# Hybrid Mamba-2 and attention step on one core: skip weights as whole rows, two first products side by side, a stacked step product, squares summed by TensorE

## The chip, the cores and the metric

The kernel runs on one core of a Trainium2 chip. The metric is the device time of one execution in microseconds (us), as the median of several. TensorE multiplies matrices, VectorE (DVE), ScalarE (ACT) and GpSimd (POOL) work on elements, and SyncE (SP) issues the DMAs, all of them on one queue.

## The reference, cut to what matters

One step of a two-layer decoder: layer 0 is a Mamba-2 mixer and an MLP, layer 1 is sliding-window attention over shared keys and values and an MLP. 1104 columns go through it together: 1024 prompt tokens, 64 sample tokens (8 sequences of 8) and 16 meta tokens, each of width 1024. The change lies in the start of the mixer:

```python
def rmsnorm(x, w):
    xf = xf * lax.rsqrt(jnp.mean(xf * xf, axis=-1, keepdims=True) + EPS)
    return (xf * w).astype(x.dtype)

def mamba_mixer(h, ...):
    zxbcdt = rmsnorm(h, norm_w) @ w_in            # 1024 -> 2048 z, 4096 x/B/C, 32 dt
    conv = conv_b
    for k in range(CONV_K):                       # 4 taps, per channel
        conv = conv + xpad[:, k:k + L] * conv_w[k]
    xbc = jax.nn.silu(conv)
    dt = jax.nn.softplus(dt_raw + dt_bias)        # the step, one per head
    y, h_new = ssd_scan(xs, dt, a_neg, bm, cm, h0)
    y = y + d_skip[head] * xs                     # the skip weights, 32 numbers
    out = gated_group_rmsnorm(y, z, gate_w) @ w_out
```

## The kernel before

Everything is held with features on the 128 partitions and tokens along the columns. The 1104 columns are cut into three chunks (`CH`): c0 and c1 of 384 columns, c2 of 336; the work on them goes in the order c2, c0, c1 (`CORD`). A width of 1024 is eight k tiles (`KT`).

Products of fp32 accuracy are made from parts. A weight or an activation is split into a high part (rounded to fp32r, by ScalarE) and a low part (the difference, by VectorE or GpSimd), and `mm3` (L179 to L181) runs three TensorE products for each k tile: high by high, high weight by low input, low weight by high input. `wunit` loads a weight tile of 512 KB (L160), casts it (L164, ScalarE) and subtracts (L165, GpSimd); it has two raw buffers and six buffers for parts.

`mixer` begins layer 0. `load_h` loads the input, four DMAs of 128x2x384 (336 for c2) fp32 numbers for each chunk (L284). `sums_x` squares them on ScalarE (L295), adds the squares of two k tiles on VectorE (L296) and sums over the partitions with a product by a matrix of 1/1024 in plain fp32 (L297); the squares go through five small buffers (`n1`). `rstd_x` makes the norm from the sums, with a logarithm (L303) and an exponential (L305) on ScalarE, each behind a table load. `norm_x` scales the eight k tiles (L316, VectorE), casts them to high parts (L317, ScalarE) and subtracts for the low parts (L319, even tiles on VectorE, odd ones on GpSimd) into the buffer `S`. The norms of c0 and c1 are written together, behind the sums of both.

A conv unit is one weight tile with its 128 output channels. `conv_mm` multiplies one chunk by it (24 products into one PSUM bank, of which a ring of three is used here) and copies the result out on ScalarE (L513, L515, L517). `conv_rest` does the taps (L533, L536), a tanh and the last product of the SiLU. The first two units are B and C of group 0; each takes c2, then c0, then c1. After them come `dt_product` (72 products with 32 output rows, the step before its bias), the units x0 and x1, `dt_path` (softplus and the running sums of the step) and the state-space groups: eight times `ssd`, 9 blocks each, with the weight loads and products of the next group (`group_in`) between its blocks. The skip weights are held as one column for each pair of heads (`dcol`, L378), read by L631 in `ssd`.

The order of the instructions on each engine is not the order of the code. A scheduler with a model of the machine orders them when the program is built; on the chip each engine works through its list in order and waits on semaphores. Eight hardware semaphores are shared in turn by SyncE's DMAs, so an issue can wait for the DMA eight places before it.

## Time and profile before

| | |
|---|---|
| time, median of 3 runs | 2992.69 us (2989.01 to 2993.91) |
| the profiled execution | 2977.05 us, span 2975.3 us |
| TensorE, share of the span | 96% |
| VectorE | 66% |
| ScalarE | 49% |
| GpSimd | 48% |
| mean granted TensorE clock | 0.984 of full speed |
| moved by DMA | 346.37 MB, mean 116 GB/s |

The span runs from the first to the last instruction; the profiled execution's time holds 1.75 us more. The three timed runs lie 12 to 17 us above the profiled execution. A busy TensorE is not TensorE at its peak, since its records overlap.

### The profile page before, as it was taken

The page shows a single profiled execution, that of the slowest core. Times are in us where ns is not written, and L with a number is a line of the kernel's source. Part 1 is how long each engine was busy: PE and PEld are TensorE (multiplying, and loading weights), DVE is VectorE, ACT ScalarE, POOL GpSimd, SP SyncE. Part 2 cuts the span into 40 slices and gives each one's busy share as a digit, 9 for nine tenths or more (in the row PEclk, how much of TensorE's full clock was granted, in tenths as well). Part 3 has the DMA queues.
Part 4 walks back from the last instruction along what each step waited for, and adds up shares of the span by engine and source line. Part 5 has one row for each costly group of instructions (what it writes and reads, how often), then busy time and mean ns, then how long its engine had stood idle before and what let it go on. Part 6 is the DMA issues. An engine that isn't in the chain of part 4 may idle for free.

```text
span 2975.3 us, 50874 instructions
## 1 busy us (share of the span) xinstructions
PE 2842.1 (96%) x19750; PEld 2728.4 (92%) x19750; DVE 1956.7 (66%) x3157; ACT 1455.1 (49%) x2770; POOL 1424.9 (48%) x1247
## 2 busy tenths in 40 slices
PE   5999999989999989999999999999988999999998
PEld 4998998979999989999999998887878999999998
DVE  5787787775565575454466766776788545366675
ACT  5455555555454465545333336566654444433333
POOL 4476666663323214444255555455543444435562
PEclk8999999999999999999999999999998999999999
DMA  3344444454212224343634312223232444543332
GB/s 126 75 120 121 126 119 120 122 149 139 68 64 71 87 71 152 134 154 124 254 131 134 115 50 65 66 74 105 86 108 97 145 136 149 186 172 128 130 110 75
DMA packets 197545, 346.37 MB, mean 116 GB/s; under 512 B 28648, under 2 KB 130920, under 8 KB 194728
## 3 DMA queue, kind: packets, MB, share of 16 engines
q1 hardware_dynamic: 197304, 343.13, 36.0%
q8 instruction: 155, 2.54, 0.4%
q14 instruction: 86, 0.70, 0.1%
HBM read 252.92 MB, written 91.12 MB: 116 GB/s over the span
## 4 chain that ended last, share of the span: by engine, by line
PE 46%; DVE 9%; ACT 4%; issue 3%; POOL 2%; DMA 1%; DVEq 0%; SPq 0%; POOLq 0%; ACTq 0%
PE g L179 4%; PE g L180 3%; PE g L181 3%; PE mc L179 3%; PE mc L181 3%; PE mc L180 3%; PE ma L179 3%; PE ma L180 3%; PE ma L181 3%; PE md L181 2%; PE md L180 2%; PE mb L179 2%; PE mb L180 2%; PE md L179 2%; PE mb L181 2%
## 5 line engine op out<-in xcount | busy, mean ns | idle before, releaser
L179 PE MATMUL g<-S,w 128*128 128x384 f32 (+3 forms) x1656 | 560.7, 339 | 16.9 <-DVE hh L729 4.8
L165 POOL TENSOR_TENSOR w<-raw,w 128x1024 fp32r<-128x1024 f32 x140 | 344.8, 2465 | 459.8 <-ACT w L164 386.6
L180 PE MATMUL g<-S,w 128*128 128x384 f32 (+3 forms) x1656 | 561.3, 339 | 3.7 <-DVE S L319 3.4
L181 PE MATMUL g<-S,w 128*128 128x384 f32 (+3 forms) x1656 | 556.0, 336 | 0.0
L859 POOL TENSOR_TENSOR w<-s,w 128x384 fp32r<-128x384 f32 (+1 forms) x240 | 324.1, 1354 | 387.1 <-ACT w L858 381.2
L179 PEld LDWEIGHTS g<-S,w 128*128 128x128 f32 (+1 forms) x1656 | 314.8, 190 | 26.3 <-issue 7.0
L859 POOL TENSOR_TENSOR w<-raw,w 128x384 fp32r<-128x384 f32 (+1 forms) x180 | 225.4, 1255 | 227.7 <-ACT w L858 204.4
L180 PEld LDWEIGHTS g<-S,w 128*128 128x128 f32 (+1 forms) x1656 | 314.8, 190 | 8.9 <-DVE S L319 4.4
L181 PEld LDWEIGHTS g<-S,w 128*128 128x128 f32 (+1 forms) x1656 | 314.8, 190 | 4.9 <-issue 2.6
L858 ACT CAST w<-s 128x384 fp32r<-128x384 f32 (+1 forms) x240 | 134.7, 562 | 243.2 <-PE ma L181 67.8
L179 PE MATMUL ma<-S,w 128*128 128x276 f32 (+1 forms) x736 | 213.4, 290 | 4.7 <-DVE us L1059 3.9
L180 PE MATMUL ma<-S,w 128*128 128x276 f32 (+1 forms) x736 | 212.8, 289 | 0.9 <-DVE S L823 0.9
L181 PE MATMUL ma<-S,w 128*128 128x276 f32 (+1 forms) x736 | 212.8, 289 | 0.0
L164 ACT CAST w<-raw 128x1024 fp32r<-128x1024 f32 x140 | 146.4, 1046 | 120.6 <-PE g L180 57.8
L729 DVE TENSOR_TENSOR hh<-hh,g 128x384 f32<-128x384 f32 (+2 forms) x264 | 134.3, 530 | 67.7 <-PE g L181 67.1
L536 DVE SCALAR_TENSOR_TENSOR fm<-xp,cv,fm 128x1024 f32<-128x1024 f32 x96 | 163.2, 1701 | 23.4 <-ACT fm L517 22.8
L858 ACT CAST w<-raw 128x384 fp32r<-128x384 f32 (+1 forms) x180 | 100.5, 561 | 151.7 <-PE mc L181 47.9
L179 PEld LDWEIGHTS ma<-S,w 128*128 128x128 f32 x736 | 139.1, 189 | 5.8 <-ACT w L858 5.7
L180 PEld LDWEIGHTS ma<-S,w 128*128 128x128 f32 x736 | 139.1, 189 | 1.1 <-DVE S L823 1.1
L181 PEld LDWEIGHTS ma<-S,w 128*128 128x128 f32 x736 | 138.9, 189 | 0.0
L179 PE MATMUL mc<-S,w 128*128 128x276 f32 (+1 forms) x464 | 134.4, 290 | 2.7 <-DVE rx L888 1.4
L181 PE MATMUL mc<-S,w 128*128 128x276 f32 (+1 forms) x464 | 134.0, 289 | 0.0
(469 smaller groups left out, 8840.3 us busy)
## 6 DMA issues: line engine op xcount, KB each, us to landing
raw<-in_w_up_dram SPq DMA_DIRECT2D x64, 512.0 KB
raw<-in_w_in_dram SPq DMA_DIRECT2D x48, 512.0 KB
raw<-in_w_downs_dram SPq DMA_DIRECT2D x64, 384.0 KB
ab<-acs_d SPq DMA_DIRECT2D x64, 256.0 KB
S<-t_d SPq DMA_DIRECT2D x18, 828.0 KB
S<-t_e SPq DMA_DIRECT2D x18, 816.0 KB
t_d<-rx SPq DMA_DIRECT2D x12, 1104.0 KB
t_e<-rx SPq DMA_DIRECT2D x12, 1088.0 KB
```

What stands on the lines that cost most here:

```text
L164: nc.scalar.copy(out=wh, in_=raw)
L165: nc.gpsimd.tensor_tensor(out=wl, in0=raw, in1=wh.bitcast(F32), op=ALU.subtract)
L179: mm(out=out, lhsT=wh, rhs=xh, start=(first and k == 0), stop=False)
L180: mm(out=out, lhsT=wh, rhs=xl, start=False, stop=False)
L181: mm(out=out, lhsT=wl, rhs=xh, start=False, stop=(k == n - 1))
L536: nc.vector.scalar_tensor_tensor(out=acc[:, :SEQ], in0=xp[:, k:k + SEQ], scalar=cv[:, j, k:k + 1], in1=acc[:, :SEQ], op0=ALU.mult, op1=ALU ...
L729: nc.vector.tensor_tensor(out=hv, in0=hv, in1=pt[:, :n], op=ALU.add)
L858: nc.scalar.copy(out=t[:, 0], in_=src)
L859: nc.gpsimd.tensor_tensor(out=t[:, 1], in0=src, in1=t[:, 0].bitcast(F32), op=ALU.subtract)
```

## The change

Five things. (1) The 32 skip weights are loaded as one row of 128 bytes to each of 128 partitions (`drow`), and GpSimd picks the 16 columns of each half; before, two DMAs read them with a stride, 64 partitions by 16 single numbers each. The input loads of c1 are written ahead of the mixer's constants. (2) For c0 and c1 the squares are no longer added in pairs on VectorE; each goes to TensorE, 16 products in place of 8. c2 keeps the addition. (3) `conv_mms` runs B and C side by side, k tile by k tile, into two banks. (4) `dt_product` stacks high and low weights in one tile of 64 columns (`wa`) and the raw weights and zeros in another (`wb`): two products for a k tile in place of three, with 64 output rows; `dt_path` adds the two halves while it transposes, by a matrix of two stacked identities (`two`). (5) The copy of 120 rows of the value cache from input to output, which has no inputs from the kernel, is held until the last up-projection weight of layer 0 has been issued.

```diff
--- before.py
+++ after.py
@@ -284,7 +284,7 @@
             self.nc.sync.dma_start(out=hp[kp], in_=self.i["x"][:, 2 * kp:2 * kp + 2, o:o + n])
         return hp
 
-    def sums_x(self, c, hp, tag):
+    def sums_x(self, c, hp, tag, add=False):
 
         nc = self.nc
         n = CH[c][1]
@@ -293,8 +293,11 @@
             sq = [self.n1("xsq")[:, :n] for _ in range(2)]
             for j in range(2):
                 nc.scalar.activation(out=sq[j], in_=h[:, j], func=AF.Square)
-            nc.vector.tensor_tensor(out=sq[0], in0=sq[0], in1=sq[1], op=ALU.add)
-            nc.tensor.matmul(out=ms[:, :n], lhsT=self.ones_d, rhs=sq[0], start=(kp == 0), stop=(kp == 3))
+            if add:
+                nc.vector.tensor_tensor(out=sq[0], in0=sq[0], in1=sq[1], op=ALU.add)
+            for j in range(1 if add else 2):
+                nc.tensor.matmul(out=ms[:, :n], lhsT=self.ones_d, rhs=sq[j], start=(kp + j == 0),
+                                 stop=(kp == 3 and (add or j == 1)))
         return ms[:, :n]
 
     def rstd_x(self, mss):
@@ -374,26 +377,30 @@
         nc.scalar.mul(out=self.cv[:, :, 0:5], in_=self.cv[:, :, 0:5], mul=0.5)
 
         self.dcol = mp.tile([P, 16], F32, name="dcol")
+        drow = mp.tile([P, 32], F32, name="drow")
+        nc.sync.dma_start(out=drow, in_=i["a_d_skip"].broadcast_to([P, 32]))
         for h in range(2):
-            nc.sync.dma_start(
-                out=self.dcol[64 * h:64 * h + 64, :],
-                in_=i["a_d_skip"].rearrange("o (t h) -> o h t", h=2)[:, h].broadcast_to([64, 16]),
-                allow_slow_non_contiguous=True)
+            hs = slice(64 * h, 64 * h + 64)
+            nc.gpsimd.tensor_copy(out=self.dcol[hs], in_=drow[hs].rearrange("p (t h) -> p h t", h=2)[:, h])
 
     def dt_product(self, mp, xs):
+
         nc, i = self.nc, self.i
         raw = self.raw([P, KT, 32])
         nc.sync.dma_start(out=raw, in_=i["w_dt"])
-        wh, wl = (self.wtile([P, KT, 32]) for _ in range(2))
-        nc.scalar.copy(out=wh, in_=raw)
-        nc.vector.tensor_tensor(out=wl, in0=raw, in1=wh.bitcast(F32), op=ALU.subtract)
-        draw = self.fm([32, T], "draw")
+        wa, wb = (self.wtile([P, KT, 64]) for _ in range(2))
+        nc.vector.memset(wb[:, :, 32:64].bitcast(F32), 0.0)
+        nc.scalar.copy(out=wa[:, :, 0:32], in_=raw)
+        nc.vector.tensor_tensor(out=wa[:, :, 32:64], in0=raw, in1=wa[:, :, 0:32].bitcast(F32), op=ALU.subtract)
+        nc.scalar.copy(out=wb[:, :, 0:32], in_=raw)
+        draw = self.fm([64, T], "draw")
         for c in CORD:
             o, n = CH[c]
-            pt = self.gps()
-            self.mm3(pt[:32, :n], [(wh[:, k], wl[:, k]) for k in range(KT)],
-                     [(xs[c][0][:, k, :n], xs[c][1][:, k, :n]) for k in range(KT)])
-            nc.scalar.copy(out=draw[:, o:o + n], in_=pt[:32, :n])
+            pt = self.gps()[:64, :n]
+            for k in range(KT):
+                nc.tensor.matmul(out=pt, lhsT=wa[:, k], rhs=xs[c][0][:, k, :n], start=(k == 0), stop=False)
+                nc.tensor.matmul(out=pt, lhsT=wb[:, k], rhs=xs[c][1][:, k, :n], start=False, stop=(k == KT - 1))
+            nc.scalar.copy(out=draw[:, o:o + n], in_=pt)
         return draw
 
     def dt_path(self, mp, draw):
@@ -413,10 +420,16 @@
         nc.sync.dma_start(out=an, in_=i["a_log"].broadcast_to([P, 32]))
         nc.scalar.activation(out=an, in_=an, func=AF.Exp)
         nc.vector.tensor_scalar(out=an, in0=an, scalar1=-1.0, scalar2=None, op0=ALU.mult)
+
+        two = mp.tile([64, 32], F32, name="two")
+        for h in range(2):
+            hs = slice(32 * h, 32 * h + 32)
+            nc.gpsimd.tensor_copy(out=two[hs], in_=self.ident[hs, hs])
         tps = ps.tile([P, 512], F32, tag="tp", name="tp")
         for t in range(9):
             n = P if t < 8 else 80
-            nc.tensor.transpose(tps[:n, t * 32:(t + 1) * 32], draw[:, t * P:t * P + n], self.ident[:32, :32])
+            nc.tensor.matmul(out=tps[:n, t * 32:(t + 1) * 32], lhsT=draw[:, t * P:t * P + n], rhs=two, start=True,
+                             stop=True)
 
         def full(f):
             f(slice(0, P), slice(0, 8))
@@ -503,12 +516,31 @@
 
     def conv_mm(self, unit, c, xs):
 
-        nc = self.nc
-        j, (wh, wl), xp, acc = unit
-        o, n = CH[c]
+        wh, wl = unit[1]
+        n = CH[c][1]
         pt = self.gps()
         self.mm3(pt[:, :n], [(wh[:, k], wl[:, k]) for k in range(KT)],
                  [(xs[c][0][:, k, :n], xs[c][1][:, k, :n]) for k in range(KT)])
+        self.conv_out(unit, c, pt)
+
+    def conv_mms(self, units, c, xs):
+
+        n = CH[c][1]
+        pts = [self.gps() for _ in units]
+        mm = partial(self.nc.tensor.matmul, skip_group_check=True)
+        for k in range(KT):
+            xh, xl = (x[:, k, :n] for x in xs[c])
+            for (j, (wh, wl), *_), pt in zip(units, pts):
+                mm(out=pt[:, :n], lhsT=wh[:, k], rhs=xh, start=(k == 0), stop=False)
+                mm(out=pt[:, :n], lhsT=wh[:, k], rhs=xl, start=False, stop=False)
+                mm(out=pt[:, :n], lhsT=wl[:, k], rhs=xh, start=False, stop=(k == KT - 1))
+        for unit, pt in zip(units, pts):
+            self.conv_out(unit, c, pt)
+
+    def conv_out(self, unit, c, pt):
+        nc = self.nc
+        j, w, xp, acc = unit
+        o, n = CH[c]
         m = min(n, SEQ - o)
         nc.scalar.copy(out=xp[:, 3 + o:3 + o + m], in_=pt[:, :m])
         if m < n:
@@ -1215,8 +1247,9 @@
         for b in range(NB):
             nc.sync.dma_start(out=o["v_s"][b, 120:128, ds], in_=self.vt[8 * b:8 * b + 8, 8, ds])
         if pr == 0:
-            nc.sync.dma_start(out=o["v_s"][:, 0:120].rearrange("b s d -> b (s d)"),
-                              in_=i["cache_v"][:, 8:128].rearrange("b s d -> b (s d)"))
+            with self.tc.issue_after(self.last_raw):
+                nc.sync.dma_start(out=o["v_s"][:, 0:120].rearrange("b s d -> b (s d)"),
+                                  in_=i["cache_v"][:, 8:128].rearrange("b s d -> b (s d)"))
 
     def keys_values(self, pr, xs, ap, buf, ps):
         yield from self.keys(pr, xs, ap, buf)
@@ -1702,20 +1735,18 @@
         hp = {2: self.load_h(2)}
         us = [self.conv_unit(0, nm) for nm in ("B", "C")]
         hp[0] = self.load_h(0)
+        hp[1] = self.load_h(1)
         self.mixer_consts(mp)
-        hp[1] = self.load_h(1)
-        ms2 = self.sums_x(2, hp[2], "cb")
+        ms2 = self.sums_x(2, hp[2], "cb", True)
         rs2 = self.rstd_x([ms2])[0]
         xs[2] = self.norm_x(2, hp[2], rs2)
         ms0 = self.sums_x(0, hp[0], "st")
         ms1 = self.sums_x(1, hp[1], "y")
-        for u in us:
-            self.conv_mm(u, 2, xs)
+        self.conv_mms(us, 2, xs)
         rs0, rs1 = self.rstd_x([ms0, ms1])
         for c, rs in ((0, rs0), (1, rs1)):
             xs[c] = self.norm_x(c, hp[c], rs)
-            for u in us:
-                self.conv_mm(u, c, xs)
+            self.conv_mms(us, c, xs)
         draw = self.dt_product(mp, xs)
         ux = self.conv_unit(0, "x0")
         fm["B"], fm["C"] = (self.conv_rest(u) for u in us)
```

What the scheduler makes of it, at three places. First SyncE's list at the very start. xt is the input, raw a weight tile, cv the conv weights and states, dtbias and an the step's bias and decay. Before:

```order
L160 DMA raw<-in_w_in_dram 128x1024 x2
L284 DMA xt<-in_x_dram 128x2x384 x4
L373 DMA cv<-in_cv_dram 128x928
L378 DMA dcol<-in_a_d_skip_dram 64x16x1 x2
L284 DMA xt<-in_x_dram 128x2x384 x4
L411 DMA dtbias<-in_a_dt_bias_dram 128x32
L413 DMA an<-in_a_log_dram 128x32
L1218 DMA out_dram<-in_cache_v_dram 8x2x15360
L386 DMA raw<-in_w_dt_dram 128x256
```

Now:

```order
L160 DMA raw<-in_w_in_dram 128x1024 x2
L284 DMA xt<-in_x_dram 128x2x384 x8
L376 DMA cv<-in_cv_dram 128x928
L381 DMA drow<-in_a_d_skip_dram 128x32
L418 DMA dtbias<-in_a_dt_bias_dram 128x32
L420 DMA an<-in_a_log_dram 128x32
L390 DMA raw<-in_w_dt_dram 128x256
```

The four loads of c1 have moved ahead of the conv weights and the skip weights, and the copy of the value cache has left this part of the list.

Second, ScalarE's list from the squares of c1 to the norm of c0 (xsq the squares, S<-xt the casts, xms the sums, n the norm). Before:

```order
L295 ACTIVATE xsq<-xt 128x384 x5
L414 ACTIVATE an<-an 128x32
L295 ACTIVATE xsq<-xt 128x384 x3
L388 CAST w<-raw 128x256
L295 ACTIVATE xsq<-xt 128x384
L303 ACT_TABLE_LOAD
L303 ACTIVATE n_359<-xms,eps 128x384
L305 ACT_TABLE_LOAD
L305 ACTIVATE n_359<-n_359 128x384
L317 CAST S<-xt 128x384 x3
```

Now:

```order
L295 ACTIVATE xsq<-xt 128x384 x3
L377 ACTIVATE cv<-cv 128x32x5
L421 ACTIVATE an<-an 128x32
L393 CAST w<-raw 128x8x32
L395 CAST w<-raw 128x8x32
L295 ACTIVATE xsq<-xt 128x384
L306 ACT_TABLE_LOAD
L306 ACTIVATE n_361<-xms,eps 128x384
L295 ACTIVATE xsq<-xt 128x384
L308 ACT_TABLE_LOAD
L308 ACTIVATE n_361<-n_361 128x384
L295 ACTIVATE xsq<-xt 128x384
```

All squares of c1 stood ahead of the norm of c0; now the norm of c0 stands between them, behind the fifth square of c1.

Third, SyncE's list in the middle of a state-space group, the second one (ab and ef are the decays that `ssd` reads back, y_d its result, raw the next group's weights). Before:

```order
L562 DMA ab<-acs_d 128x4x128
L566 DMA ef<-eacs_d 64x2x128 x2
L562 DMA ab<-acs_d 80x4x80
L160 DMA raw<-in_w_in_dram 128x1024
L635 DMA y_d_80<-yt 256x1x128
L566 DMA ef<-eacs_d 64x2x128 x2
```

Now:

```order
L667 DMA y_d_80<-yt 256x1x128
L594 DMA ab<-acs_d 80x4x80
L598 DMA ef<-eacs_d 64x2x128 x2
L667 DMA y_d_80<-yt 256x1x128
L594 DMA ab<-acs_d 128x4x128
L160 DMA raw<-in_w_in_dram 128x1024
```

The weight load stood right behind the decays of the tail block (80x4x80); now two loads of ef, a store of y_d and one more ab stand between them. Such shifts of a few places run through the groups; behind the mixer the lists are the same but for the copy of the value cache.

## Rows read from the trace of the kernel before

**Rows 1.** The page's part 1 (busy time, share of the span and instructions of each engine), and, below the dots, the longest entry of the waits of TensorE over the whole span (engine and line that waited, what it waited for: us in total, times, longest us):

```profile
PE 2842.1 (96%) x19750; PEld 2728.4 (92%) x19750; DVE 1956.7 (66%) x3157; ACT 1455.1 (49%) x2770; POOL 1424.9 (48%) x1247
...
PE xms L297 <- DVE xsq L296: 23.6, 4, 8.7
```

**Rows 2.** Busy time of each engine in stretches of the first 85 us (stretch, its length, then for each engine the busy us and, in brackets, its instructions; PEclk is the granted TensorE clock as a share of full speed; then DMA share and GB/s):

```profile
0.00:28.80 28.80, 13.88 (x36) 8.22 (x36) 14.64 (x24) 16.16 (x32) 13.49 (x32) 1.00 0.47 157
28.80:37.50 8.70, 0.00 (x0) 0.00 (x0) 0.56 (x1) 1.49 (x4) 0.00 (x0) 0.71 0.73 238
47.20:56.30 9.10, 4.63 (x13) 3.97 (x14) 9.02 (x15) 8.32 (x16) 7.31 (x10) 0.63 0.01 3
64.50:72.80 8.30, 8.25 (x47) 8.26 (x48) 3.55 (x6) 2.67 (x5) 2.53 (x2) 1.00 0.36 126
72.80:85.00 12.20, 12.20 (x75) 7.97 (x74) 11.40 (x7) 4.44 (x7) 4.67 (x4) 1.00 0.30 87
```

**Rows 3.** The timeline of SyncE's DMA issues in the first 60 us (start, time that the issues took, line, what is loaded, how many):

```profile
4.24 2.97 SPq L284 DMA_DIRECT2D xt<-in_x_dram  x4
8.29 4.05 SPq L378 DMA_DIRECT2D dcol<-in_a_d_skip_dram  x2
12.39 19.55 SPq L284 DMA_DIRECT2D xt<-in_x_dram  x4
33.42 0.84 SPq L1218 DMA_DIRECT2D out_dram<-in_cache_v_dram  x1
```

**Rows 4.** The DMA engines between 12 and 36 us in 40 equal slices of 0.6 us: busy tenths, GB/s, and below the packets by size:

```profile
DMA  9999710000000000000000000000022242469999
GB/s 382 379 394 404 198 32 7 0 0 0 0 0 0 0 0 0 0 0 0 0 0 0 0 0 0 0 0 0 13 69 75 85 69 82 151 226 351 381 726 394
DMA packets 3613, 2.66 MB, mean 111 GB/s; under 512 B 2273, under 2 KB 3480, under 8 KB 3608
```

**Rows 5.** What the DMA engines moved between 0 and 10 us:

```profile
DMA packets 1641, 2.64 MB, mean 264 GB/s; under 512 B 239, under 2 KB 1388, under 8 KB 1641
```

**Rows 6.** The timeline of ScalarE in the first 60 us (start, us, line, operation, how many; in brackets the idle time before it and what ended that). L295 squares the input, L303 and L305 are the logarithm and the exponential of the norm, each behind its table load:

```profile
14.89 1.75 ACT L295 ACTIVATE xsq<-xt 128x384 f32<-128x384 f32 x4
35.94 1.95 ACT L295 ACTIVATE xsq<-xt 128x384 f32<-128x384 f32 x4 [13.31 <-DMA xt<-in_x_dram]
44.77 0.58 ACT L303 ACTIVATE n<-xms,eps 128x384 f32<-128x384 f32 x1
45.37 1.28 ACT L305 ACT_TABLE_LOAD   x1
46.66 0.52 ACT L305 ACTIVATE n<-n 128x384 f32<-128x384 f32 x1
54.49 1.28 ACT L305 ACT_TABLE_LOAD   x1
55.79 0.52 ACT L305 ACTIVATE n<-n 128x384 f32<-128x384 f32 x1
```

**Rows 7.** The timeline of VectorE, the same columns. L316 scales the input by the norm, L319 forms the low part of every other k tile:

```profile
15.76 5.84 DVE L316 SCALAR_TENSOR_TENSOR xt<-xt,nv,n 128x336 f32<-128x336 f32 x8
47.22 5.06 DVE L316 SCALAR_TENSOR_TENSOR xt<-xt,nv,n 128x384 f32<-128x384 f32 x8 [3.13 <-ACT n L305]
56.34 7.26 DVE L316 SCALAR_TENSOR_TENSOR xt<-xt,nv,n 128x384 f32<-128x384 f32 x8
63.95 2.78 DVE L319 TENSOR_TENSOR S<-xt,S 128x384 fp32r<-128x384 f32 x4
```

**Rows 8.** The timeline of TensorE, the same columns. A matmul's own duration includes its pipeline, so the time from one start to the next is what it costs in a stream. L297 sums the squares (two records to one product), L179 to L181 are the three products of mm3:

```profile
44.81 0.81 PE L297 MATMUL xms<-xsq,ones_r 128*128 128x384 f32 x2
45.16 0.61 PE L181 MATMUL g<-S,w 128*128 128x336 f32 x1
53.61 0.52 PE L179 MATMUL g<-S,w 128*128 128x384 f32 x1
53.93 0.52 PE L180 MATMUL g<-S,w 128*128 128x384 f32 x1
64.55 0.44 PE L180 MATMUL g<-S,w 128*128 128x384 f32 x1 [1.67 <-DVE S L319]
84.91 0.32 PE L179 MATMUL g<-S,w 128*128 128x336 f32 x1
```

**Rows 9.** Groups of instructions of the first 70 us, shapes kept apart (line, engine, operation, tiles, shape, count | busy us, mean ns of one | idle us before them and its releaser):

```profile
L295 ACT ACTIVATE xsq<-xt 128x384 f32<-128x384 f32 x16 | 7.5, 513 | 14.0 <-DMA xt<-in_x_dram 13.3 <-DVE xsq L296 0.6
L317 ACT CAST S<-xt 128x384 fp32r<-128x384 f32 x16 | 8.1, 513 | 2.8 <-DVE xt L316 2.7
L513 ACT COPY xp<-g 128x256 f32<-128x256 f32 x2 | 0.7, 360 | 0.0
L515 ACT COPY xp<-g 128x80 f32<-128x80 f32 x2 | 0.5, 236 | 0.0
L517 ACT ACTIVATE fm<-g,cv 128x336 f32<-128x336 f32 x2 | 1.3, 646 | 0.0
```

**Rows 10.** The waits between 70 and 700 us (us in total, times, longest us): the longest of TensorE, then of SyncE's queue and of ScalarE those on the weights:

```profile
PE st L666 <- POOL bm L654: 7.3, 4, 2.7
...
SPq L160 <- POOL w L165: 57.0, 16, 12.7
...
ACT w L164 <- PE g L180: 28.4, 18, 4.8
```

## The prediction

> **What bounds the kernel now.** I read the page first: TensorE is busy for 96% of the span, so a change pays if it shortens what TensorE does or closes a hole in its work. The waits of TensorE say where holes are: the longest entry by far, 23.6 us in four times, is L297, the sum of squares, waiting for VectorE's added squares [rows 1]. That stands in the first 45 us, so I cut the start into stretches. Between 28.8 and 37.5 TensorE does nothing, and VectorE and ScalarE next to nothing; from 47.2 to 56.3 it is half busy; from 64.5 on it is busy all the time [rows 2]. The products of B and C end at about 72.8, those of the step at 84.91, where x0 starts (128x336 again) [rows 8].
>
> What is late at 28.8? ScalarE waits 13.31 us for the input of c1 and squares it from 35.94 [rows 6]. SyncE's timeline shows why the data are late. c0's four issues took 2.97 us together; the two skip-weight DMAs come next, from 8.29 to 12.34, and the four issues of c1 behind them took 19.55 us [rows 3]. In that time the DMA engines stood idle from about 15 to 29 us, and when they moved again they were only 0.2 busy for five slices; 2273 packets of the stretch are under 512 bytes, and the skip weights are 2 x 64 x 16 = 2048 separate numbers [rows 4]. So the 8 KB of skip weights held the queue, and c1's 1.5 MB stood behind them.
>
> **The change, part by part.** *Loads.* To the end of c1 the queue now carries nv 32 KB, c2 1344, two weight tiles 1024, c0 and c1 1536 each: 5.60 MB. 2.64 MB had passed at 10 us [rows 5]; the full slices run at about 390 GB/s [rows 4], so c1 is there at 10 + 2.96/0.39 = 17.6 us, not 35.9. The conv weights, the skip rows, bias, decay and step weights follow within some 2 us. From then on not the data but the engines' lists bound the start; I follow the list that is last at each step.
>
> *To the norm of c0.* VectorE scales c2 from 15.76 to 21.60 as before, and its first low part takes some 0.6 more (c1's four took 2.78) [rows 7]: 22.15. For this the product list of TensorE waits. In the new list 12 products of c2 and then the sum of c0's last square stand there; the fifth square of c1 needs that sum done (a ring of five buffers), and the norm of c0 stands behind that square. TensorE is cold after its pauses: a 384-column product took 0.32 us start to start at 53.61, so one of 336 takes 0.28; the plain-fp32 sum took 0.35 at full clock (44.81 to 45.16), so 0.64 cold [rows 8]. 22.15 + 12 x 0.28 + 0.64 = 26.2. Behind it on ScalarE: a square 0.51 [rows 9], a table load 1.28 and the logarithm 0.58, a square 0.51, a table load 1.28 and the exponential 0.52 [rows 6]: 30.9. Before, the scaling of c0 began at 47.22 [rows 7].
>
> Those two records of L297 are two passes over 384 columns. The Trainium skill's page "FP8 and Floating Point Precision" (TensorE Precision Notes) counts four passes for true fp32; by it the sum in this chain would take 1.28 us cold and the gain below would be 0.6 us smaller. The two records and 0.35 us decide here.
>
> *To the products of c1.* Eight scalings took 5.06 us for c0, mostly with GpSimd idle, and 7.26 for c1 beside GpSimd's low parts [rows 7]; in the new order c0's odd low parts run beside it, so I take 6.2, between them: 37.1. The last cast 0.51 [rows 9], then table load, logarithm, table load, exponential, 1.28 + 0.58 + 1.28 + 0.52 [rows 6]: 41.3. The scaling of c1 7.26: 48.5. In the trace TensorE went on 0.95 us after that (63.60 to 64.55) [rows 7, 8]: 49.5, against 64.55. That is 15.0 us earlier.
>
> Two waits are new here. B and C of c0 need two banks; one of them is B's of c2, which ScalarE now empties only after the norm of c1, so C of c0 starts at 41.3 + 0.36 + 0.24 + 0.65 = 42.5 [rows 9]. B's 23 products fill the time from 38.1 to about 43, and C's 25 end by about 48, still ahead of 49.5. And the weight buffers of x0 and x1 come free only as B and C end together; the step's products, 8 us, cover the subtraction on GpSimd. Without that cover it would cost some 3 us.
>
> *Products of the step.* 75 products took 12.2 us from 72.8 to 85.0 [rows 2], 0.163 each. 24 fewer: 3.9 us. Nothing waits for anything else there, so it comes off the span.
>
> *At nothing.* Eight added products for the squares cost 2.8 us at full clock, within TensorE's waits for c0; their additions go from a VectorE that waits for ScalarE. The fill of `wb`, one more cast of 0.4 us, the copies of `two` and of the skip columns lie where VectorE and GpSimd wait. Nine small products in place of nine transposes: under 1 us, taken as 0. The value-cache copy, 1 MB, moves to the end of an up-projection where nothing of the page waits for loads; at 390 GB/s it is 2.5 us of DMA, bound 0 to 3.
>
> Sum: 15.0 less one product more to do behind it, 0.2, plus 3.9 = 18.7 us. The profiled execution took 2977.05 us; it would take 2958.3. The timed runs lie 15.6 us above it by their median; nothing in the change touches that, so 2992.7 - 18.7 = 2974 us. Bounds of the sum: with TensorE warm in the chain (0.155 for each of the 12, 0.35) and c0's scaling at 5.06 it is 21.6; the cold case below gives 7.7. The groups of the mixer are reordered too; TensorE's largest wait between 70 and 700 us is 7.3 us in four times [rows 10], so I allow 4 us either way.
>
> **The rivals.** *Cold start.* TensorE ran at a granted clock of 0.63 between 47.2 and 56.3, where it had paused [rows 2], and a 384-column product cost 0.32 there against 0.18 later. In the new order it pauses again between c2 and c0. If all of c0 and c1 ran at 1.2 GHz, c0 would take 48 x 0.32 = 15.4 from 38.1, ending at 53.5 in place of 49.5, and c1 15.4 in place of 8.4: 11 us lost, a gain of 7.7, 2985 us. Against it: the products of c1 ran warm in the trace, right behind c0's. The Trainium skill's page "TensorE: Matmul & The Clock Gate" (What's actually happening) says that the throttled clock is the default and activity lifts it, which the trace's start bears out; by that rule pauses left in the start cost more than their own length. Chance 12%.
>
> *The hole stays.* c1's loads could be slow for another reason, the depth of the queue behind c0. Then only the step's 3.9 us and a little on VectorE remain: 2988 us. The idle DMA engines and the small packets right behind the skip weights speak against it. 6%.
>
> *More.* The reordered groups wait less, and the chain runs at its fast bound: 2967 us, 8%.
>
> *Slower.* In each of seven groups the four weight loads stand some places later on SyncE, behind stores and decays that wait for VectorE. If each came late by more than 24.7/28 = 0.9 us beyond its slack (18.7 of gain plus 6), the time would be over 2998.7; at 1.2 us each, 2992.7 - 18.7 + 33.6 = 3008. Against it: a load is issued when GpSimd frees a raw buffer, 57.0 us of SyncE's waits, two units ahead, and the cast waits for TensorE to free a buffer, not for data [rows 10]. 4%.
>
> **The numbers.** The sum as worked out has 70%. Range 2964 to 2986: its fast bound with 4 us more from the groups, rounded outward, and the cold case; it leaves out the hole that stays, the slow case and a little on either side. The likeliest case alone: 2969 to 2979. A measurement of this kernel can tell 0.2%, 6 us, from no change. Faster by that: the sum, the cold case and more, less a tail of 3%: 87%. Same: the hole that stays and most of that tail, 8%. Slower 5%.
>
> **What would show it.** In the changed profile c1's eight issues take about 0.7 us each and no slice of the DMA engines is empty before 18 us; the scaling of c0 starts near 31 and that of c1 near 41; x0's first product near 66 us (84.91 before), 48 products of the step in about 8 us ahead of it; the groups' waits near those of before. I am wrong if c1 still lands after 30 us, if the products of c0 and c1 stand 0.32 us apart throughout, or if the gain at x0 is gone by 700 us, where waits of the groups for weights or decays would name the place.

## The result, and the profile after

The changed kernel took 2971.85 us (median of 4 runs, 2965.84 to 2973.85) beside 2990.85 us for the kernel before on the same chip (2986.70 to 2993.91): a ratio of 0.9934, 95% interval 0.9914 to 0.9954, 19.0 us between the medians. The forecast was 2974.0, a gain of 18.7. The sum came out; two of its terms did not, and a loss that nobody had costed hid it.

The profiled execution took 2972.13 us, span 2970.4. That is only 4.9 us less than the span before, because the kernel before was profiled in an execution 10 us faster than any of the four timed beside the changed one.

The page's first line, and the wait of the first 70 us that answers to the 23.6 us of [rows 1] (us in total, times, longest). It is the one ahead of the very first sum, which the kernel before has too (6.29 of its 23.6); the others are gone:

```profile
PE 2848.8 (96%) x19751; PEld 2733.9 (92%) x19751; DVE 1945.4 (65%) x3150; ACT 1452.5 (49%) x2771; POOL 1419.9 (48%) x1251
```

```profile
PE xms L299 <- DVE xsq L297: 6.4, 1, 6.4
```

SyncE's timeline of the changed kernel (start, us of the issues, line, what):

```profile
4.42 6.78 SPq L284 DMA_DIRECT2D xt<-in_x_dram  x8
12.94 0.34 SPq L381 DMA_DIRECT2D drow<-in_a_d_skip_dram  x1
16.17 0.33 SPq L390 DMA_DIRECT2D raw<-in_w_dt_dram  x1
```

Its DMA engines between 12 and 36 us, in slices of 0.6 us (busy tenths, GB/s):

```profile
DMA  9999999999999774300009494000000001000000
GB/s 371 376 369 379 371 374 374 371 374 395 402 342 324 290 261 194 137 21 0 0 0 109 164 403 178 21 14 0 0 0 0 0 0 27 0 0 0 0 0 0
```

Eight input loads are issued in 6.78 us, where c1's four alone took 19.55 [rows 3], and the hole of the DMA engines from 15 to 29 us [rows 4] is gone: they are full until 20 us, and little is left to load when they fall idle at 22. ScalarE's logarithms and exponentials for c0 and c1 (L306, L308):

```profile
26.15 0.58 ACT L306 ACTIVATE n<-xms,eps 128x384 f32<-128x384 f32 x1
28.45 0.53 ACT L308 ACTIVATE n<-n 128x384 f32<-128x384 f32 x1
37.47 0.58 ACT L306 ACTIVATE n<-xms,eps 128x384 f32<-128x384 f32 x1
39.36 0.53 ACT L308 ACTIVATE n<-n 128x384 f32<-128x384 f32 x1
```

VectorE's scalings of c0 and c1:

```profile
29.01 6.60 DVE L319 SCALAR_TENSOR_TENSOR xt<-xt,nv,n 128x384 f32<-128x384 f32 x8 [5.11 <-ACT n L308]
39.92 4.33 DVE L319 SCALAR_TENSOR_TENSOR xt<-xt,nv,n 128x384 f32<-128x384 f32 x8 [1.46 <-ACT n L308]
```

TensorE's timeline: the first product of a low part of c2, of c1, the first step product and the first product of x0:

```profile
21.50 0.42 PE L535 MATMUL g<-S,w 128*128 128x336 f32 x1 [2.04 <-DVE S L322]
...
46.77 0.44 PE L535 MATMUL g<-S,w 128*128 128x384 f32 x1 [1.11 <-DVE S L322]
...
55.58 0.31 PE L401 MATMUL g<-S,w 128*64 128x336 f32 x1
...
63.58 0.32 PE L179 MATMUL g<-S,w 128*128 128x336 f32 x1
```

x0 starts at 63.58, against 84.91 [rows 8]: 21.3 us earlier. TensorE in the first stretches (busy us of PE first; the third number from the end is the granted clock), to be read against [rows 2]:

```profile
0.00:28.80 28.80, 17.50 (x60) 10.75 (x61) 11.69 (x23) 22.82 (x45) 14.56 (x36) 1.00 0.74 254
28.80:37.50 8.70, 7.42 (x39) 6.04 (x38) 8.49 (x12) 6.08 (x13) 5.31 (x5) 1.00 0.01 2
```

The stretch that was empty is full, at a granted clock of 1.00.

Where the 21.3 us went afterwards is told by a comparison of whole traces: for each instruction of VectorE, ScalarE and GpSimd that both kernels have, how much earlier it starts than in the profile of the kernel before, as the median of a stretch of 100 us from the time given (x0 by its first product, the end by the spans). Negative is earlier.

| kernel | x0 | 600 | 1400 | 1700 | 2200 | end | time, ratio to before (95%) |
|---|---|---|---|---|---|---|---|
| changed | -21.3 | -26.1 | -24.2 | -15.9 | -6.5 | -4.9 | 0.9934 (0.9914 to 0.9954) |
| changed, again | -20.8 | -25.8 | -23.4 | -15.6 | -11.3 | -9.4 | 0.9926 (0.9903 to 0.9948) |
| e1 row only | -14.1 | -14.3 | -12.0 | -12.7 | -11.5 | -10.1 | 0.9947 (0.9930 to 0.9965) |
| e2 order only | +2.6 | +2.7 | +5.1 | +4.6 | +9.3 | +9.5 | 1.0003 (0.9993 to 1.0014) |
| e3 strided twice | +17.5 | +21.7 | +23.0 | +22.9 | +26.5 | +26.7 | 1.0054 (1.0038 to 1.0070) |
| e4 old loads | -6.2 | -10.3 | -9.0 | -2.1 | +5.8 | +6.3 | 0.9978 (0.9966 to 0.9990) |
| e5 one by one | -21.9 | -26.6 | -25.0 | -17.8 | -7.4 | -6.4 | 0.9943 (0.9921 to 0.9965) |
| e6 added squares | -16.4 | -21.9 | -21.9 | -23.2 | -14.7 | -14.4 | 0.9921 (0.9901 to 0.9941) |
| e7 old step | -18.1 | -17.0 | -17.6 | -12.3 | -1.6 | +0.5 | 0.9959 (0.9945 to 0.9973) |
| e8 early copy | -19.2 | -23.8 | -23.2 | -18.0 | -16.9 | -14.9 | 0.9923 (0.9906 to 0.9940) |
| e9 both | -17.4 | -23.3 | -23.6 | -24.0 | -24.2 | -23.9 | 0.9895 (0.9875 to 0.9916) |
| e10 copy behind x1 | -19.6 | -24.0 | -22.7 | -15.9 | -10.3 | -10.4 | 0.9919 (0.9900 to 0.9937) |
| e12 squares only | -0.6 | +0.7 | +0.4 | +6.6 | +9.3 | +10.8 | 0.9998 (0.9986 to 1.0011) |

The changed kernel gains 21.3 us by x0 and 5 more in the mixer's groups, and loses 8 between 1400 and 1700 us (layer 0's down-projection) and 9 between 1700 and 2200 (attention). A kernel that took the time of the one before (e2, e12) ends some 10 us behind the profile of the kernel before, so about 10 of each late difference belong to that one execution; what counts is how the rows differ among themselves.

### The profile page after: what moved, and what is told of

Read it like the earlier page. It is cut to its first block, busy times and chain, and to the rows that moved or that the text cites. A ratio compares the mean times of both kernels' runs of the same rounds, so it can differ in the third digit from the quotient of the medians.

```text
span 2970.4 us, 50898 instructions
## 1 busy us (share of the span) xinstructions
PE 2848.8 (96%) x19751; PEld 2733.9 (92%) x19751; DVE 1945.4 (65%) x3150; ACT 1452.5 (49%) x2771; POOL 1419.9 (48%) x1251
## 4 chain that ended last, share of the span: by engine, by line
PE 37%; DVE 12%; DMA 5%; ACT 4%; issue 4%; POOL 3%; DVEq 0%; ACTq 0%; POOLq 0%; SPq 0%
PE g L179 4%; PE g L180 4%; PE g L181 4%; PE mc L179 2%; PE mc L181 2%; PE mc L180 2%; PE ma L179 2%; PE ma L180 2%; PE ma L181 2%; DMA t_e<-rx 2%; POOL w L891 2%; PE md L181 2%; PE md L180 2%; PE md L179 2%; PE mb L180 2%
## 5 line engine op out<-in xcount | busy, mean ns | idle before, releaser
L165 POOL TENSOR_TENSOR w<-raw,w 128x1024 fp32r<-128x1024 f32 x140 | 352.9, 2523 | 437.5 <-ACT w L164 355.3
L179 PE MATMUL g<-S,w 128*128 128x384 f32 (+2 forms) x1584 | 535.3, 338 | 14.1 <-DVE hh L761 4.8
L180 PE MATMUL g<-S,w 128*128 128x384 f32 (+2 forms) x1584 | 534.5, 337 | 0.1
L181 PE MATMUL g<-S,w 128*128 128x384 f32 (+2 forms) x1584 | 531.1, 336 | 2.0 <-POOL w L165 2.0
L179 PEld LDWEIGHTS g<-S,w 128*128 128x128 f32 x1584 | 302.1, 191 | 18.9 <-DVE hh L761 5.1
L181 PEld LDWEIGHTS g<-S,w 128*128 128x128 f32 x1584 | 302.2, 191 | 3.5 <-POOL w L165 2.3
L180 PEld LDWEIGHTS g<-S,w 128*128 128x128 f32 x1584 | 302.3, 191 | 1.8 <-issue 0.7
L179 PE MATMUL ma<-S,w 128*128 128x276 f32 (+1 forms) x736 | 214.6, 292 | 9.8 <-DVE us L1091 6.6
L181 PE MATMUL ma<-S,w 128*128 128x276 f32 (+1 forms) x736 | 213.7, 290 | 0.0
L568 DVE SCALAR_TENSOR_TENSOR fm<-xp,cv,fm 128x1024 f32<-128x1024 f32 x96 | 161.1, 1680 | 33.1 <-ACT fm L549 32.5
L179 PEld LDWEIGHTS ma<-S,w 128*128 128x128 f32 x736 | 139.9, 190 | 11.3 <-issue 5.2
L181 PEld LDWEIGHTS ma<-S,w 128*128 128x128 f32 x736 | 139.8, 190 | 0.0
L179 PE MATMUL mc<-S,w 128*128 128x276 f32 (+1 forms) x464 | 134.6, 290 | 2.1 <-DVE hh L1091 1.3
L181 PE MATMUL mc<-S,w 128*128 128x276 f32 (+1 forms) x464 | 134.0, 289 | 0.0
```

Of the source, the lines that this page charges most:

```text
L165: nc.gpsimd.tensor_tensor(out=wl, in0=raw, in1=wh.bitcast(F32), op=ALU.subtract)
L179: mm(out=out, lhsT=wh, rhs=xh, start=(first and k == 0), stop=False)
L180: mm(out=out, lhsT=wh, rhs=xl, start=False, stop=False)
L181: mm(out=out, lhsT=wl, rhs=xh, start=False, stop=(k == n - 1))
L568: nc.vector.scalar_tensor_tensor(out=acc[:, :SEQ], in0=xp[:, k:k + SEQ], scalar=cv[:, j, k:k + 1], in1=acc[:, :SEQ], op0=ALU.mult, op1=ALU ...
```

## The experiments

**The loads: e1 to e4.** The theory: 2048 single numbers hold the queue. The rival: the depth of the queue does.

*e1, the row alone.* `mixer_consts` of the kernel before with

```diff
+        drow = mp.tile([P, 32], F32, name="drow")
+        nc.sync.dma_start(out=drow, in_=i["a_d_skip"].broadcast_to([P, 32]))
         for h in range(2):
-            nc.sync.dma_start(out=self.dcol[64 * h:64 * h + 64, :], in_=..., allow_slow_non_contiguous=True)
+            hs = slice(64 * h, 64 * h + 64)
+            nc.gpsimd.tensor_copy(out=self.dcol[hs], in_=drow[hs].rearrange("p (t h) -> p h t", h=2)[:, h])
```

> The kernel before with one edit: the skip weights come as one row per partition and GpSimd copies the columns; c1's loads stay behind the conv weights and the skip weights, and nothing else changes (the order on TensorE, VectorE and ScalarE is that of the kernel before). Theory (the 2048 separate numbers hold the queue): c1 is there before 20 us; ScalarE was free for its squares at 22.63 us (35.94 less the 13.31 it waited), so everything behind moves 13.3 us up: the logarithm of c0 at about 31.5 (44.77 before), x0's first product at 71.6 (84.91 before), time about 13 us under the kernel before. Rival (the hole stays, depth of the queue): c1's squares at 35 to 36 again, x0 at 84 to 85, no gain.

Measured: 2970.46 us beside 2987.22 us. TensorE's first product of x0:

```profile
70.83 0.32 PE L179 MATMUL g<-S,w 128*128 128x336 f32 x1
```

As the theory had it (71.6). One edit brings two thirds of what the whole change has gained at x0, and as a time it cannot be told from the changed kernel (0.9947 and 0.9934 of the kernel before, intervals that overlap).

*e2, the order alone.*

```diff
-        self.mixer_consts(mp)
         hp[1] = self.load_h(1)
+        self.mixer_consts(mp)
```

> The kernel before with one edit: c1's four loads are issued ahead of the conv weights and of the skip weights, which are still read as 2048 separate numbers. Theory: the skip weights then hold only what stands behind them (bias, decay, step weights, x0's weights), and none of it is needed before some 55 us; so the same 13.3 us as with the row alone, x0 at about 71.6, and the row by itself adds nothing to the order. If the single numbers slow whatever is near them, or the depth of the queue decides, x0 stays at 80 to 85 and the gain under 5 us.

Measured: 2986.50 us, no gain, x0 at 87.55. The expectation was wrong by 16 us. ScalarE:

```profile
26.73 0.51 ACT L295 ACTIVATE xsq<-xt 128x384 f32<-128x384 f32 x1
40.59 0.23 ACT L414 ACTIVATE an<-an 128x32 f32<-128x32 f32 x1 [13.35 <-DMA an<-in_a_log_dram]
...
45.24 0.41 ACT L388 CAST w<-raw 128x256 fp32r<-128x256 f32 x1 [2.45 <-DMA raw<-in_w_dt_dram]
```

c1's squares no longer wait for c1. But the exponential of the decay, 32 numbers, stands between them in ScalarE's list, its load stands behind the skip weights on SyncE, and 13.35 us of waiting moved there from c1's 13.31 [rows 6]. That the result is not needed before 55 us does not help: the list is worked in order. So the hole is still there, and my reading of what it harms was too narrow: it harms whatever is next in the queue and is read by an engine whose list the start hangs on.

*e3, the strided loads twice.*

```diff
-        for h in range(2):
+        dtwo = mp.tile([P, 16], F32, name="dtwo")     # read by nothing
+        for h in range(4):
+            dst = (dtwo, self.dcol)[h // 2]
+            h = h % 2
             nc.sync.dma_start(
-                out=self.dcol[64 * h:64 * h + 64, :],
+                out=dst[64 * h:64 * h + 64, :],
                 ...
```

> The kernel before, with the two strided DMAs of the skip weights issued twice (once more into a tile that nothing reads), ahead of c1's loads. Theory: the idle time of the DMA engines, some 14 us, doubles; c1's squares start at 50 to 55 us in place of 35.94, x0 at 99 to 104, time 14 to 19 us over the kernel before. Rival (depth of the queue): two more issues in a queue, 1 to 2 us, x0 at 85 to 87.

Measured: 3002.31 us, 15.1 over the kernel before, x0 at 102.41. SyncE (two pairs of strided loads, then c1's input) and ScalarE's first square of c1:

```profile
8.34 3.97 SPq L381 DMA_DIRECT2D dtwo<-in_a_d_skip_dram  x2
12.35 13.91 SPq L381 DMA_DIRECT2D dcol<-in_a_d_skip_dram  x2
26.31 24.97 SPq L284 DMA_DIRECT2D xt<-in_x_dram  x4
```

```profile
55.11 2.55 ACT L295 ACTIVATE xsq<-xt 128x384 f32<-128x384 f32 x5 [32.47 <-DMA xt<-in_x_dram]
```

8 KB more of single numbers cost 19 us of c1's loading (55.11 against 35.94) and 15 us of the time. Depth of the queue is out: two more issues were to cost 1 to 2 us by it.

*e4, the changed kernel with the old loads* (e1's edit and e2's undone; the second is shown):

```diff
-        hp[1] = self.load_h(1)
         self.mixer_consts(mp)               # with the two strided loads again
+        hp[1] = self.load_h(1)
```

> The changed kernel with the loads of the kernel before: strided skip weights ahead of c1's loads; squares by TensorE, products side by side, stacked step weights and the late copy of the value cache stay. Theory: the hole comes back; c1's squares start near 36, the logarithm of c0, which stands behind five of them, near 40 (26.15 in the changed kernel), x0 near 78 (63.58), time 13 to 15 us over the changed kernel, some 5 under the kernel before. If the other parts carried the gain, x0 would be under 70 and the time within 5 us of the changed kernel.

Measured: 2980.53 us beside 2987.22 us, x0 at 78.74: the hole is back and costs 15.2 us at x0, as expected. What is left of the gain, 6.2 us at x0, is the other parts'.

**The other parts of the start: e5 to e8.** *e5, B and C one after the other*, at all three chunks:

```diff
-            self.conv_mms(us, c, xs)
+            for u in us:
+                self.conv_mm(u, c, xs)
```

> The changed kernel, with the first products of B and C again one unit after the other. The theory costs the side-by-side order at nothing: both are 48 products for a chunk, and TensorE waits for the norms either way. x0's first product at 63 to 65 us (63.58 in the changed kernel), time within 2 us of it. Rival: one after the other, C of c0 waits for its bank and B ends a chunk early, or c1's first products fill holes worse, and x0 comes 2 to 4 us later.

Measured: 2970.12 us beside 2984.54 us, x0 at 63.06. Side by side is worth nothing that shows here.

*e6.*

```diff
-        ms0 = self.sums_x(0, hp[0], "st")
-        ms1 = self.sums_x(1, hp[1], "y")
+        ms0 = self.sums_x(0, hp[0], "st", True)
+        ms1 = self.sums_x(1, hp[1], "y", True)
```

> The changed kernel, with the squares of c0 and c1 added in pairs by VectorE again, 8 products in place of 16. The theory costs this part at nothing, 2.8 us of TensorE against 8 additions of VectorE, both in waits: x0 between 63 and 66 us, time 0 to 2 us over the changed kernel. Rival: VectorE's list puts the additions behind the scaling of c2, the squares' ring stalls on them as in the kernel with the row alone (ScalarE waited 0.62 to 1.79 us for them five times, some 4.4 us), and x0 comes 3 to 5 us later.

Measured: 2961.73 us beside 2984.54 us, x0 at 68.53. At the start the rival was right: ScalarE's squares wait for VectorE's additions to free the ring,

```profile
22.90 0.52 ACT L295 ACTIVATE xsq<-xt 128x384 f32<-128x384 f32 x1 [0.70 <-DVE xsq L297]
24.07 1.06 ACT L295 ACTIVATE xsq<-xt 128x384 f32<-128x384 f32 x2 [0.65 <-DVE xsq L297]
26.22 0.53 ACT L295 ACTIVATE xsq<-xt 128x384 f32<-128x384 f32 x1 [1.09 <-DVE xsq L297]
...
29.59 0.94 ACT L295 ACTIVATE xsq<-xt 128x384 f32<-128x384 f32 x2 [0.63 <-DVE xsq L297]
```

and x0 comes 4.9 us later. Of these, 3.4 us stand at c1's logarithm already (40.91 against 37.47); behind it a granted clock of 0.50 from 39.6 to 46.4 us adds to them. Yet the whole is not slower, since the loss of 8 us between 1400 and 1700 us is missing (the table). That was expected by nobody, and e9 and e12 look into it.

*e7, the old step product*, with the transposes of the kernel before (the products are shown, not the weights):

```diff
-                nc.tensor.matmul(out=pt, lhsT=wa[:, k], rhs=xs[c][0][:, k, :n], start=(k == 0), stop=False)
-                nc.tensor.matmul(out=pt, lhsT=wb[:, k], rhs=xs[c][1][:, k, :n], start=False, stop=(k == KT - 1))
+            self.mm3(pt[:32, :n], [(wh[:, k], wl[:, k]) for k in range(KT)],
+                     [(xs[c][0][:, k, :n], xs[c][1][:, k, :n]) for k in range(KT)])
```

> The changed kernel with the step product of the kernel before: three products for a k tile, 72 in all, and the transposes. With it the order of the mixer's groups goes back to that of the kernel before. Theory of the prediction: 24 products more, x0 3.9 to 4.2 us later, at 67.6. The groups gained another 5 us by 1050 us in the changed kernel (21 us ahead at x0, 26 there), while the kernels with the old step kept their lead unchanged over the groups (14.0 at x0, 14.3 at 600 us with the row alone); if that comes from the new order, it is lost here too, and the time is 8 to 10 us over the changed kernel; if it came from the start alone, 4 us.

Measured: 2973.31 us beside 2984.54 us. x0 at 66.81, 3.2 us later: the 72 products take 12.0 us from their first, at 54.81, where the 48 take 8.0, but they start 0.8 us earlier. By 600 us the lead is 17.0, not 26.1. TensorE's waits between 70 and 700 us, first in e7, then in the changed kernel:

```profile
PE st L689 <- POOL bm L677: 7.2, 4, 2.7
PE st L689 <- DVE hT L664: 4.4, 1, 4.4
```

```profile
PE tp L602 <- ACT Bt L610: 3.1, 4, 1.5
PE cb L614 <- DVE cbm L616: 3.0, 5, 1.5
PE st L698 <- DVE hT L673: 1.7, 3, 0.7
```

With the old step the groups are ordered as before and have the waits of before (7.3 us for `bm` stood in [rows 10]). With the stacked one the scheduler places the group's work otherwise, these waits are gone and smaller ones stand there: some 6 us where the prediction had allowed 4. In the table all eight kernels with the stacked product gain 4.1 to 5.9 us between x0 and 600 us, and none of the five with the old one gains more than 0.2. By the ratios e7 takes 7 to 10 us more than the changed kernel, as the order had been expected to cost.

*e8, the copy of the value cache early.*

```diff
-            with self.tc.issue_after(self.last_raw):
-                nc.sync.dma_start(out=o["v_s"][:, 0:120]..., in_=i["cache_v"][:, 8:128]...)
+            nc.sync.dma_start(out=o["v_s"][:, 0:120]..., in_=i["cache_v"][:, 8:128]...)
```

> The changed kernel with the 1 MB copy of the value cache back at the head of SyncE's list, ahead of the step weights, in place of behind layer 0's last up-projection weight (issued at 1364 us). The prediction costed the late copy at 0 to 2.5 us. The changed kernel fell back by 8 us between 1490 and 1660 us, as did the one with the strided loads and all else changed; the three with the early copy did not. If the late copy costs it: no such fall here, time 6 to 10 us under the changed kernel, 2962 to 2966, less what the copy costs at the start, 0 to 3 us. If the fall is the clock's, 0.97 there: time within 2 us of the changed kernel.

Measured: 2962.47 us beside 2984.54 us, x0 at 65.71. The time is one that "the late copy costs it" had named, but the kernel before was 6 us quicker in this comparison too: by the ratios e8 is 1 to 3 us under the changed kernel, within the intervals, where 6 to 10 had been named. The fall between 1400 and 1700 us is still there (5.2 us), the one in attention is not. Nor are the 2.1 us at x0 shown to be the copy's: c1's logarithm starts at 37.22, as early as in the changed kernel, and behind it TensorE has the low clock for 3.5 us, which at half speed is 1.7 us lost:

```profile
47.80:51.30 3.50, 3.16 (x10) 3.16 (x11) 2.93 (x6) 0.89 (x2) 1.14 (x1) 0.51 0.26 40
```

**The two late falls: four more runs.** The changed kernel again, with no edit:

> The changed kernel, unchanged, profiled a second time. In its first profile it led the kernel before by 26 us at 1050 us and by 5 at the end; 8 us went between 1480 and 1690 us (layer 0's down-projection, TensorE waiting 4.6 us for hh and 4.8 for us of L1091) and 9 between 2030 and 2160 (attention, a granted clock of 0.51 from 2024 to 2034). If these belong to the program, the same waits and the same slow stretch stand here again, x0 starts at 63.6, and the time is within 3 us of the first result. If they were that one execution's, at least one of the two is gone.

Measured: 2965.04 us beside 2986.11 us; both falls, the second smaller.

e9 is e6's edit and e8's together:

> The changed kernel with two parts undone: squares of c0 and c1 added by VectorE, and the copy of the value cache at the head of SyncE's list. The kernels with the squares on TensorE all fell back by 5 to 8 us in layer 0's down-projection, those with added squares did not; the kernels with the late copy all fell back by 6 to 9 us in attention, those with the early copy by 0 to 3. If each fall belongs to its part: x0 at about 70.6 (63.6, 4.9 for the additions, 2.1 for the copy), neither fall, and 3 to 5 us under the kernels with one of them undone. If the falls come by chance from how transfers and the clock meet, the time lies anywhere between those and the changed kernel.

Measured: 2956.89 us (2951.27 to 2961.33) beside 2986.11, x0 at 67.47: neither fall, and the fastest kernel of the study, 8.2 us under the changed kernel in the same comparison, though it starts x0 3.4 us later. x0 had been expected at 70.6, with 2.1 us for the copy; against e6 (68.53) the early copy costs nothing here.

e10 holds the copy, but only until x1's weights have been issued (`x1_raw` is that load; how it is found is left out):

```diff
-            with self.tc.issue_after(self.last_raw):
+            with self.tc.issue_after(self.x1_raw):
```

> The changed kernel with the copy of the value cache held until the weights of x1 have been issued, so behind all that the start needs, but some 1300 us earlier than in the changed kernel. The start is that of the changed kernel, x0 at 63.6. If the late place of the copy costs the 8 us in attention, they are gone: 8 to 10 us under the changed kernel, and 2 under the one with the copy at the head. If the fall in attention is chance, or comes with any copy that is held, the time is that of the changed kernel.

Measured: 2963.14 us beside 2986.11, the time of the changed kernel. The fall in attention is there without the late copy (15.9 to 10.3), and x0 is at 65.32 though the start's lists are those of the changed kernel. TensorE from 21.4 us, in e10 and in the changed kernel:

```profile
21.40:24.00 2.60, 2.18 (x11) 2.18 (x12) 2.60 (x6) 2.60 (x8) 2.01 (x4) 0.78 0.12 48
24.00:28.00 4.00, 4.00 (x16) 3.00 (x15) 0.22 (x1) 2.00 (x4) 0.28 (x1) 0.72 0.63 239
```

```profile
21.40:24.00 2.60, 2.50 (x15) 2.35 (x15) 2.50 (x6) 2.35 (x8) 2.29 (x4) 1.00 0.12 47
24.00:28.00 4.00, 4.00 (x18) 2.82 (x17) 0.00 (x0) 3.64 (x5) 0.00 (x0) 1.00 0.44 133
```

In e10 the clock fell to the low level right in the chain to c0's norm; in the changed kernel it did not. The prediction's chain had been reckoned cold throughout; on the chip either happens.

e12 is the kernel before with the squares on TensorE (`sums_x` of the changed kernel), with the lists behind the first 85 us unchanged:

```diff
-            nc.vector.tensor_tensor(out=sq[0], in0=sq[0], in1=sq[1], op=ALU.add)
-            nc.tensor.matmul(out=ms[:, :n], lhsT=self.ones_d, rhs=sq[0], start=(kp == 0), stop=(kp == 3))
+            if add:                         # c2 alone
+                nc.vector.tensor_tensor(out=sq[0], in0=sq[0], in1=sq[1], op=ALU.add)
+            for j in range(1 if add else 2):
+                nc.tensor.matmul(out=ms[:, :n], lhsT=self.ones_d, rhs=sq[j], start=(kp + j == 0), ...)
```

> The kernel before with one edit: the squares of c0 and c1 go to TensorE unadded. All lists behind the first 85 us are those of the kernel before. c1 still lands at 36 us; from there to the logarithm of c0 the kernel before took 8.8 us, the changed kernel's squares with the old loads 6.0, so x0 comes 2.8 us earlier, at 82. If the squares on TensorE bring the fall in layer 0's down-projection, it shows between 1480 and 1690 us here too, and the time is 3 to 5 us over the kernel before; if not, some 3 us under it.

Measured: 2988.24 us beside 2986.11 us, no difference. c0's logarithm comes 3.1 us earlier (41.66), but x0 only 0.6 (84.36). The fall in layer 0's down-projection is there: from 0.4 to 6.6 us behind, and every engine's list behind the first 85 us is that of the kernel before.

*The fall in the down-projection* thus goes with one edit. All eight profiles of kernels with the squares on TensorE have it, none of the six with added squares (the kernel before, e1, e2, e3, e6, e9). TensorE's waits between 1480 and 1690 us, in the changed kernel and in e9:

```profile
PE ma L179 <- DVE us L1091: 4.8, 2, 2.5
PE mb L179 <- DVE hh L1091: 4.6, 1, 4.6
```

```profile
PE mb L179 <- DVE hh L1091: 3.3, 1, 3.3
PE ma L179 <- DVE us L1091: 2.0, 2, 1.0
```

That is 4.1 us more of waits in the changed kernel, half of the 8 that it loses; the granted clock there is lower too, 0.98 against 0.99 over some 300 us. What is late there? Two loads of `R` feed ScalarE's casts (L1058). In the second profile of the changed kernel and in e9 these were issued at 1456.36 and 1456.16:

```profile
1464.53 1.58 ACT L1058 CAST R<-R 128x1656 fp32r<-128x1656 f32 x1 [1.92 <-DMA R<-t_d]
```

```profile
1462.97 1.58 ACT L1058 CAST R<-R 128x1656 fp32r<-128x1656 f32 x1 [0.49 <-DMA R<-t_d]
```

8.17 us from issue to cast against 6.81; over all profiles 8.1 to 8.5 against 6.75 to 7.1, with no overlap. The bytes and the order of the issues are the same. The lead goes in five or six steps of about 1 to 2 us up to 1680 us, and this late load is the first of them. One thing differs: the queue that brings instructions to the core. Its share between 1461.5 and 1463.5 us in the changed kernel, and between 1463.5 and 1465.5 in e9 (in each the other stretch has none):

```profile
q8 instruction: 1, 0.02, 3.0%
```

```profile
q8 instruction: 1, 0.02, 3.2%
```

3.0% of 16 engines in 2 us is 0.96 us of one engine, inside the load in the one kernel and behind it in the other. The other profiles fit: in all eight with the late load this fetch starts 5.8 to 6.4 us behind the load's issue, in the other six 7.3 to 8.2, when the load has landed. Eight more products near the start shift TensorE's place in its instruction stream, which may be what moves the fetch. No run moves the fetch alone, so the link to the edit is shown and the instruction fetch is a guess.

*The fall in attention* goes with no single edit: it stands in e10 and e12 without the late copy, and not in e8 or e9. The instruction lists are the same there, but for the copy. TensorE from 2014 us in the changed kernel, then from 2004 us in its second profile, then from 2022 us in the kernel before:

```profile
2014.00:2024.00 10.00, 6.55 (x48) 5.99 (x48) 6.70 (x12) 5.60 (x15) 8.34 (x5) 1.00 0.36 122
2024.00:2034.00 10.00, 10.00 (x58) 8.53 (x58) 4.75 (x17) 4.13 (x12) 3.54 (x3) 0.51 0.59 185
```

```profile
2004.00:2014.00 10.00, 8.43 (x41) 7.17 (x40) 3.56 (x7) 6.88 (x12) 8.01 (x5) 0.70 0.29 94
2014.00:2024.00 10.00, 10.00 (x73) 9.13 (x72) 6.08 (x12) 3.55 (x9) 8.69 (x5) 0.96 0.45 145
```

```profile
2022.00:2032.00 10.00, 9.62 (x46) 8.29 (x47) 3.24 (x12) 5.72 (x6) 7.49 (x4) 0.66 0.39 114
```

The first two are the same program: once TensorE is busy for 6.55 of 10 us and then gets 0.51 of its clock, the level of 1.2 GHz, for the next ten; once it is slowed twenty earlier and back at 0.96 by then. But the kernel before is slowed here as well, so this stretch is not the fall. The fall lies 50 us further on. There a product into `yb` waits for ScalarE, and behind it the clock is low. The wait and the clock in the changed kernel, then the clock in its second profile, then the stretch in e9 that answers to both, at full clock:

```profile
2071.55 0.27 PE L1335 MATMUL yb<-ident,es 128*32 128x128 f32 x1 [1.81 <-ACT es L1302]
```

```profile
2072.00:2079.00 7.00, 7.00 (x44) 4.99 (x43) 5.00 (x17) 3.98 (x12) 0.38 (x2) 0.52 0.01 2
```

```profile
2069.50:2076.30 6.80, 6.80 (x36) 5.48 (x37) 4.27 (x14) 3.19 (x11) 0.20 (x2) 0.50 0.01 2
```

```profile
2036.00:2076.00 40.00, 38.12 (x322) 31.10 (x322) 29.41 (x105) 27.86 (x81) 11.95 (x15) 1.00 0.19 60
```

Nine of the fourteen profiles have this wait of 1.7 to 1.9 us with the low clock behind it, and lose 4.2 to 5.9 us there: all six with the late copy, and e2, e10 and e12. The other five have neither wait nor loss: the kernel before, e1, e3, e8 and e9. Why the wait comes in some and not in others is open; that the late copy makes it likelier is neither shown nor ruled out. e2 and e12 took the time of the kernel before and have it, so it may be that only the quick profile of that kernel lacks it.

## Why the prediction was right, and where it was not

**The loads: right.** The eight issues took 6.78 us, 0.85 each where about 0.7 was forecast. No DMA slice was to be empty before 18 us, and none was (the first in which nothing moves starts at 22.8). And e1, e3 and e4 show cause and size: 14.1 us for the row alone, 15.0 forecast for an earlier c1.

**The chain to c1: right in its steps, each a little quicker.** The 12 products and the sum were reckoned cold, 0.28 and 0.64; they ran at 0.155 and 0.35, and c2's first low part came at 21.50 in place of 22.15, so c0's logarithm started at 26.15, 1.85 before the reckoned 28.0. c0's scaling took 6.60 (6.2 taken), c1's 4.33 (7.26 taken, beside GpSimd; in the new order GpSimd's low parts come after it). c1's first low-part product came at 46.77, not 49.5, and behind VectorE's low part, not behind the scaling. That is the 2.6 us between 21.3 and 18.7 at x0. Eight sums more were within waits, and the two records of 0.35 us held: at 24.72 a sum of 384 columns leaves two records, 0.81 us from its start to its end, and the next product starts 0.35 us after it. The Trainium skill's page "FP8 and Floating Point Precision" (TensorE Precision Notes) counts four passes for true fp32; the trace again has two records.

**The step product: right at its place, too small in its reach.** 48 products took 8.0 us, as forecast, and e7's 72 took 12.0: 4.0 us for 3.9, of which 3.2 show at x0. But the edit also reordered the groups, and that brought 4 to 6 us more. The prediction had seen the reordering, put it at nothing with 4 us allowed either way, and called what happened the rival *More*, at 8%: by 1400 us the changed kernel was 24 us ahead.

**"At nothing" failed for the squares.** The step put both sides in waits. At the start the additions were in the ring's way: taking them out gave 3.4 us at c1's logarithm and 4.9 at x0 (e6), though under the old loads only 0.6 at x0 (e12). Then the same edit cost 5 to 8 us some 1500 us later, at a place that it does not touch (e12, e9). Neither was in the sum, and they nearly cancel. For the copy, bounded at 0 to 3, no run shows a gain: the 2.1 us of e8 at x0 go with its clock, and e9 starts x0 earlier than e6. A cost of its late place is not shown either.

**The cold start** was the main rival. It did not come in the changed kernel, whose granted clock shows 1.00 for the whole start; e10 shows it in small, 1.2 to 1.7 us at x0. Late in the kernel it came: 0.52 from 2072 to 2079 us, behind a wait of 1.81. The Trainium skill's page "TensorE: Matmul & The Clock Gate" (What's actually happening) has an idle TensorE throttled and activity lift the throttle, and calls it variable from run to run how many products at a kernel's start run slow. The two profiles of the changed kernel show the like far behind the start: 0.51 in one from 2024 to 2034 us, 0.70 and 0.96 in the other from 2004 to 2024.

So the total was right by 0.3 us partly by luck: 2.6 us more on the chain and 4 to 6 more in the groups, against 5 to 8 lost in the down-projection and, it may be, something in attention. The sign did not hang on it: the loads alone gave 16.8 us (e1).

## What to carry to other kernels

A load of single numbers on a shared queue costs not its bytes but everything that stands behind it: look for idle DMA engines next to thousands of small packets, and load a row. Moving the wanted load ahead is not the same, for an engine with an in-order list may still hang on some small load left behind (e2). And an edit of a few instructions on the busiest engine can move transfers far away by a microsecond each: compare two kernels over the whole run, and judge a gain by several variants rather than by one total.

## What had not been expected of the hardware

Eight more products on TensorE in the first 45 us went with a load 1400 us later that took 8.1 to 8.5 us from its issue to its use in all eight profiles, against 6.75 to 7.1 in the six without them; e12 shows it with the same order of instructions on every engine from 85 us on. And two pairs of strided loads, 16 KB, held c1's squares back to 55.11 us, one pair to 35.94: 19 us for 8 KB.
